# Gated DeltaNet and RWKV-7 step on one core: the first pair's key product moves among the gates' segments, and the convolution's tiles get a pool of their own

## The chip, the core and the metric

The kernel runs on one core of a Trainium2 chip. The metric is the device time of one execution in microseconds. A core has TensorE (PE in the profile; PEld are its weight loads), VectorE (DVE), ScalarE (ACT), GpSimd (POOL) and SyncE (SP), which here issues all DMAs from one queue, in order. Matrix products land in PSUM, which has eight banks; everything else lies in SBUF.

## The reference, cut to what matters

A two-layer trunk: a gated DeltaNet layer, then an RWKV-7 layer, on a prompt of 1024 + 16 tokens and on 8 sample sequences of 8 tokens, 1104 tokens in all. Only the first layer's beginning matters here.

```
xn = rmsnorm(x, norm_w)                      # 1104 tokens x 1024
proj = xn @ w_in                             # q, k, v (4096 columns), z (2048), b and a (16 + 16)
qkv, new_buf = causal_conv(qkv, conv_buf, conv_w)      # 4 taps per channel, then silu
q, k = l2norm(...), l2norm(...)              # 8 heads of 128
beta = sigmoid(b);  g = -exp(a_log) * softplus(a + dt_bias)
# per chunk of 64 tokens:
gc = cumsum(g);  decay = exp(gc_i - gc_j) for i >= j
A = I + strict_lower((k * beta) k^T * decay)
sol = triangular_solve(A, [v * beta, k * beta * exp(gc)])
# then a scan over the chunks with the state S
```

There are 8 key heads and 16 value heads, so one key head and its two value heads make a *pair* j = 0 to 7.

## The kernel before, in words

**Input.** Nine row tiles of x (128 tokens x 1024, `x0` to `x8`; the last has 80) are loaded. `input_norm` (L280) takes them in groups of two or three: sums of squares on ACT, a power on POOL, the scaling on DVE (L296). Then PE transposes each tile in eight blocks, ACT rounds the result to a high part (L305) and DVE takes the low part (L309). High and low parts lie in `xa` and `xc`, features by tokens. The x tiles lie in a pool `inp` on SBUF's right side, which is closed behind the norm.

**Products.** Every product of the projection has 128 output columns (the gates' 64) and runs over the 1104 tokens in three segments of 384, 384 and 336 (`SEGS`). A segment is 24 matmuls: 8 tiles of features by three terms (high x high, low weight x high, high x low). `product` (L438) does a segment in two halves of 12 and yields after each: a half is a *slot*. It also loads the next product's weights (`raw_weights`, L422) and splits them in segments 1 and 2 (`next_weights`: high part on ACT, low part on POOL, L87 and L91).

**Gates.** `gates` (L350) does the product of b and a in three segments, with a copy of each into `rows` (L362), yields, turns the rows into columns (`fgt`), forms beta and g with ACT and DVE, yields, makes the running sums with PE (`fgc`), yields, turns them back (`fgr`) and stores them in DRAM (`drow`). From `drow` a pair's decays E are loaded (`decays`, L649), masked on POOL (L653, L658) and turned into exponentials on ACT.

**Convolution.** `conv` (L496) is what a product hands each segment to: ACT copies the PSUM into `raw` (L546, L547, L550), multiplies by the first tap into `cvy`, and DVE adds three taps (L526). ACT takes a tanh and DVE forms the silu (L532) into K, Q or a value tile. The three old rows of the samples come from `history`: four DMAs (L475) into `hist`, a transposition on PE into the single PSUM bank `m` and a copy into `histT` (`history_turn`, L479). `hist`, `histT`, `last`, `raw` and `cvy` are tiles of the pool `gfront`, which opens when `inp` has closed and lies in the same room.

**Chain of pair 0.** From K and E come the scores (`fsc` on PE, L702 to L712 on DVE) of three segments. Their diagonal blocks of 32 go through DRAM (`ltd`, L718; `invA`, L729) into an inverse of 31 steps with two DVE instructions each (L573, L575), whose result goes through DRAM again (`g_t`, `g_u`, `T1n`) to PE's merges (`rY`, L767 the copy). Only then the scan over the chunks of pair 0 can start.

**Order.** In `layer0` (L2134) everything up to the first slot is ordered by a planner, by readiness in a simulated run and by the order in the text. From L2199 on the orders of PE and ACT are written out by hand: slots are counted, from -24 for the key product of pair 0, and `gdn_events` (L923) and `front_events` (L997) hang each step at a slot: pair 0's E is loaded at -18.5 to -18.3, its exponentials are taken from -16 on, its scores at -15.2, -14.4 and -13.6, its inverse at -11.5 and on, the merges from 2.5 on. The gates' last three parts hang at -23.4, -21.4 and -20.4. DVE, POOL and SP are ordered by the planner everywhere. All engines run their own orders strictly in sequence.

Of the kernel before, what the change touches and what calls it, by code (L numbers as in the profile page):

```python
# [14 lines left out]
D = 1024  # L15
# [21 lines left out]
class Builder:  # L37
# [229 lines left out]
    def input_open(self):  # L267
        self.inp = ExitStack()
        self.lp = self.inp.enter_context(self.tc.tile_pool(name="inp", bufs=1, side="right", reuse_waits="tile"))
        self.xrows = []  # L270

    def input_load(self, qs):
        for q in qs:
            x = self.t(self.lp, [128, D], f"x{q}")
            self.xrows.append((x, self.rows_of_x(x, q)))
            if q == 0:
                self.nwb = self.t(self.lp, [128, D], "nwb")
                self.nc.sync.dma_start(self.nwb, self.i["norm_w"][0].rearrange("(o d) -> o d", o=1).broadcast_to([128, D]))
# [71 lines left out]
    def gates(self, xh, xl):  # L350
        nc, i, t, gp = self.nc, self.i, self.t, self.gatep
        al, wz, rows, upto, past, part = self.gate_in
        nea = t(gp, [128, 16], "nea")
        self.act(nea, al[:, 0], AF.Exp)
        nc.vector.tensor_scalar(nea, nea, -1.0, None, op0=ALU.mult)
        whi = t(gp, [128, 8, 64], "whi2", dt=F32R)
        wlo = t(gp, [128, 8, 64], "wlo2", dt=F32R)
        self.split(wz, whi, wlo)
        w = ([whi[:, 0:4, :], whi[:, 4:8, :]], [wlo[:, 0:4, :], wlo[:, 4:8, :]])
        for s, (c0, n) in enumerate(SEGS):  # L360
            p = self.dense(w, 64, xh, xl, s)
            nc.scalar.copy(rows[:, c0:c0 + n], p[0:48, 0:n])  # L362
        yield
        col = self.col
        p = self.ps("f", 2, "gt")
        for k in range(9):
            self.transpose(p[:, 48 * k:48 * k + 48], rows[:, 128 * k:128 * k + 128])
        pv = p[:, 0:432].rearrange("p (k x) -> p k x", x=48)
        b, x, y, g = [t(gp, [128, 9, 16], n) for n in ("gb", "gx", "gy", "g")]
        nc.vector.tensor_tensor(x, pv[:, :, 32:48], al[:, 1].unsqueeze(1).broadcast_to([128, 9, 16]), op=ALU.add)  # L370
        nc.vector.scalar_tensor_tensor(y, x, -1.0, x, op0=ALU.mult, op1=ALU.max)
        self.act(y, y, AF.Exp, scale=-1.0)
        self.act(b, pv[:, :, 0:16], AF.Tanh, scale=0.5)
        self.act(y, y, AF.Ln, bias=1.0)
        nc.vector.scalar_tensor_tensor(y, x, 0.0, y, op0=ALU.max, op1=ALU.add)
        nc.vector.tensor_tensor(g, y, nea.unsqueeze(1).broadcast_to([128, 9, 16]), op=ALU.mult)
        gs = t(gp, [128, 9, 16], "gs")
        nc.vector.tensor_tensor(gs, g[:, 0].unsqueeze(1).broadcast_to([128, 9, 16]), part.unsqueeze(2).broadcast_to([128, 9, 16]), op=ALU.mult)
        nc.vector.tensor_scalar(col[:, :, 0, :], b, 0.5, 0.5, op0=ALU.mult, op1=ALU.add)
        yield  # L380
        flat = lambda a: a.rearrange("p k h -> p (k h)")
        p = self.ps("f", 2, "gc")
        for a, m in ((0, upto), (144, past)):
            self.mm(p[:, a:a + 16], m[0], g[:, 0])
            self.mm(p[:, a + 16:a + 144], m[1], flat(g[:, 1:9]))
        c, d = (p[:, a:a + 144].rearrange("p (k h) -> p k h", h=16) for a in (0, 144))
        gc = t(gp, [128, 144], "gc")
        nc.vector.tensor_copy(gc.rearrange("p (j k h) -> p k j h", j=8, h=2), c.rearrange("p k (j h) -> p k j h", h=2))
        e = self.ps("m", 1, "ge")
        self.mm(e[:, 0:144], self.ones, flat(gs))  # L390
        self.mm(e[:, 144:272], self.ones, flat(g[:, 1:9]))
        self.act(col[:, :, 1, :], c, AF.Identity, scale=-1.0)
        self.act(self.eglb.rearrange("p h c -> p c h"), e[:, 0:272].rearrange("p (c h) -> p c h", h=16), AF.Exp)
        self.act(col[:, :, 2, :], c, AF.Exp)
        self.act(col[:, :, 3, :], d, AF.Exp)
        yield
        p = self.ps("f", 2, "gr")
        self.transpose(p[:, 0:128], gc[:, 0:128])
        self.transpose(p[0:16, 128:256], gc[:, 128:144])
        r = t(gp, [128, 256], "gr")  # L400
        nc.vector.tensor_copy(r[:, 0:128], p[:, 0:128])
        nc.vector.tensor_copy(r[0:16, 128:256], p[0:16, 128:256])
        self.drow = self.dram([8, 9, 2, 128], "drow")
        d = self.drow.rearrange("j t h k -> (j t h) k")
        nc.sync.dma_start(d[0:128], r[:, 0:128])
        nc.sync.dma_start(d[128:144], r[0:16, 128:256])
# [62 lines left out]
    def history(self, j):  # L469

        nc, t = self.nc, self.t
        H = Ctx()
        r = t(self.fp, [108, 128], "hist", 1)[0:96]
        for u, ft in enumerate((8 + j, j, 16 + 2 * j, 17 + 2 * j)):
            nc.sync.dma_start(r[24 * u:24 * u + 24], self.i["state_gdn_conv"][0].rearrange("b r c -> (b r) c")[:, ft * 128:(ft + 1) * 128])  # L475
        H.raw = r
        return H

    def history_turn(self, H):  # L479
        p = self.ps("m", 1, "hist")  # L480
        self.transpose(p[:, 0:96], H.raw)
        H.old = self.t(self.fp, [128, 4, 8, 3], "histT", 1)
        self.nc.vector.tensor_copy(H.old.rearrange("p u b r -> p (u b r)"), p[:, 0:96])

    def last_tokens(self, j, H):
        nc = self.nc
        p = self.ps("f", 2, "last")
        self.transpose(p[0:108, 0:128], H.last.rearrange("p u b -> p (u b)"))
        ls = self.t(self.fp, [108, 128], "hist", 1)
        nc.vector.tensor_copy(ls, p[0:108, 0:128])  # L490
        for u, ft in enumerate((8 + j, j, 16 + 2 * j, 17 + 2 * j)):
            c = slice(ft * 128, (ft + 1) * 128)
            nc.sync.dma_start(self.o["s_gdn_conv"][0].rearrange("b r c -> (b r) c")[:, c], ls[27 * u:27 * u + 24])
            nc.sync.dma_start(self.o["p_gdn_conv"][0, 0][:, c], ls[27 * u + 24:27 * u + 27])

    def conv(self, H, u, ft, dst):  # L496

        nc, t = self.nc, self.t
# [2 lines left out]

        def begin():
            if u == 0:
                H.last = t(self.fp, [128, 4, 27], "last", 1)
            raws[0] = raw = t(self.fp, [128, 411], "raw", 3)
            sv = raw[:, 0:88].rearrange("p (b r) -> p b r", r=11)
            nc.vector.tensor_copy(sv[:, :, 0:3], H.old[:, u])
            nc.gpsimd.memset(raw[:, 88:91], 0.0)

        def follow(s, wd):  # L510
            prev = raws[s][:, wd:wd + 3]
            if s < 2:
                raws[s + 1] = t(self.fp, [128, 411], "raw", 3)
                nc.gpsimd.tensor_copy(raws[s + 1][:, 0:3], prev)
            else:
                nc.gpsimd.tensor_copy(H.last[:, u, 24:27], prev)

        def taps(s, wd, y):
            raw = raws[s]
            if s == 0:  # L520
                sv = raw[:, 0:88].rearrange("p (b r) -> p b r", r=11)
                nc.gpsimd.tensor_copy(H.last[:, u, 0:24].rearrange("p (b r) -> p b r", r=3), sv[:, :, 8:11])
            y.append(t(self.fp, [128, 408], "cvy", 2))
            self.act(y[0][:, 0:wd], raw[:, 0:wd], AF.Identity, scale=cw[0])
            for k in range(1, 4):
                nc.vector.scalar_tensor_tensor(y[0][:, 0:wd], raw[:, k:k + wd], cw[k], y[0][:, 0:wd], op0=ALU.mult, op1=ALU.add)  # L526
# [1591 lines left out]
    def build(self):  # L2118
        nc, tc = self.nc, self.tc
        with self.ctx as top:  # L2120
            self.input_open()
            self.input_load((0, 1, 2))
            self.consts()
# [10 lines left out]
    def layer0(self, top, right, xa, xc):  # L2134
# [7 lines left out]
        gates = ExitStack()  # L2142
        self.input_load(range(3, 9))
        self.gates_open(gates)
        self.input_norm(hi, lo)
        self.inp.close()
        self.gdn_front(front)
        self.raw_weights(1024)
        self.wnew = [], []
        self.next_weights(0)  # L2150
        self.next_weights(1)
# [2 lines left out]
        self.vectors()  # L2154
        kh, kl = [h[:, k] for h in hi for k in range(4)], [l[:, k] for h in lo for l in h for k in range(l.shape[1])]
        rows = [xa[:, k] for k in range(6)] + [xc[:, k] for k in range(10)]
        gate = self.gates(kh, kl)
        next(gate)
        G = [None] * 8

        def open_(j):
# [5 lines left out]
            self.gp = pool("gdn", ctx)  # L2167
        open_(0)
        self.history_turn(G[0].H)
        self.gdn_zero()  # L2170
        self.gdn_events(G, open_, lambda: next(gate, None), swap)

        def products():
# [12 lines left out]
                        i, h = j - 1 + h // 2, h % 2  # L2186
                        todo.append((4096 + 128 * (2 * i + h), lambda w, i=i, h=h: self.gdn_gate(i, G[i], h, kh, kl, w)))
            for n, (_, f) in enumerate(todo):
                yield from f(todo[n + 1][0] if n + 1 < len(todo) else None)

        def before(u):
            while True:
# [2 lines left out]
                    return  # L2195
                for f in self.events.pop(v):
                    f()
        before(-24)
        with tc.manual_schedule(engines={mybir.EngineType.PE, mybir.EngineType.Activation}):  # L2199
            self.slot = -24  # L2200
            for _ in products():
                before(self.slot + 1)
                self.slot += 1
        self.slot = None
        front.close()
        before(999)
        xbp = pool("xb", right, side="right")
        xb = [t(xbp, [128, 1113], f"xb{k}") for k in range(8)]
# [345 lines left out]
```

## Time and profile before

| | |
|---|---|
| three timed runs, median (lowest to highest) | 2180.25 us (2178.22 to 2181.9) |
| the profiled execution | 2173.21 us |
| its span | 2171.5 us, 54811 instructions |
| PE / DVE / ACT / POOL busy in the span | 94% / 73% / 59% / 38% |
| mean granted TensorE clock | 0.982 of full speed |
| DMA | 292.52 MB, 135 GB/s |

A page shows one profiled execution. Names like `dk<-xa,whi` are out<-in with the buffer numbers left out: `d` is the PSUM bank of a product, with `k`, `q` or `v` behind it for whose; without a letter it is here the gates'. `f`, `m` and `r` are other PSUM banks. Idle time of an engine is put down to what ended it. Matmul records overlap, since matmuls are pipelined. The times in the lines of a timeline are the start from the span's beginning and the length, and consecutive instructions of a group are merged into one line with a count.

### The profile page before, as it was taken

What the parts mean: (1) busy time and instruction counts of PE and PEld (TensorE: products, weight loads), DVE (VectorE), ACT (ScalarE), POOL (GpSimd) and SP (SyncE); (2) the same over time, 40 slices, a digit from 0 to 9 for tenths busy, and PEclk for the clock granted to TensorE, in tenths of its full rate; (3) what the DMA queues carried; (4) which work ended last, traced back from release to release, by engine and by line L of the source; (5) the groups of instructions that cost most, each with busy time, mean ns of one, the idle gap of its engine ahead of it and who ended that gap; (6) DMA issues with size and microseconds to landing.
All of it is one profiled execution on the core that took longest, in us unless ns stands there. A gap on an engine that the chain in (4) does not pass through costs nothing. (4 is left out here: it accounts for less than half of the span.)

```text
span 2171.5 us, 54811 instructions
## 1 busy us (share of the span) xinstructions
PE 2046.2 (94%) x20418; PEld 1905.8 (88%) x20418; DVE 1583.4 (73%) x4212; ACT 1283.1 (59%) x3750; POOL 834.9 (38%) x1136
## 2 busy tenths in 40 slices
PE   6969899999999999999999999889899999999997
PEld 5959899999999999998899999889798988888876
DVE  6968879698888979795334676757979557767755
ACT  4536565656565665656533365664747446677774
POOL 3523334334343333334231352344524254444444
PEclk9979999999999999999999999999999999999999
DMA  3424343424333333335345115655555486677754
GB/s 120 122 58 105 77 108 90 118 79 107 90 97 106 106 97 104 97 102 159 106 129 135 63 54 191 220 160 174 169 180 158 117 224 175 188 234 225 228 178 139
DMA packets 430724, 292.52 MB, mean 135 GB/s; under 512 B 147337, under 2 KB 413050, under 8 KB 430458
## 3 DMA queue, kind: packets, MB, share of 16 engines
q1 hardware_dynamic: 430458, 289.02, 46.2%
q8 instruction: 161, 2.64, 0.5%
q14 instruction: 105, 0.86, 0.1%
HBM read 197.55 MB, written 91.37 MB: 133 GB/s over the span
## 5 line engine op out<-in xcount | busy, mean ns | idle before, releaser
L91 POOL TENSOR_TENSOR wlo<-wraw,whi 128x512 fp32r<-128x512 f32 (+1 forms) x246 | 331.1, 1348 | 465.6 <-ACT whi L87 413.9
L77 PE MATMUL d<-xc,whi 128*128 128x384 f32 (+2 forms) x1006 | 279.5, 337 | 4.8 <-ACT whi L87 4.1
L526 DVE SCALAR_TENSOR_TENSOR cvy<-raw,cw,cvy 128x408 f32<-128x408 f32 (+2 forms) x288 | 199.0, 692 | 17.1 <-ACT cvy L63 15.7
L87 ACT CAST whi<-wraw 128x512 fp32r<-128x512 f32 (+1 forms) x246 | 149.8, 611 | 88.1 <-PE d L77 51.2
L77 PEld LDWEIGHTS d<-xc,whi 128*128 128x128 f32 (+1 forms) x1006 | 183.4, 189 | 7.8 <-ACT whi L87 4.8
L77 PE MATMUL d<-xc,wlo 128*128 128x384 f32 (+3 forms) x476 | 157.7, 340 | 2.7 <-POOL wlo L91 2.7
L77 PE MATMUL dz<-xc,whi 128*128 128x384 f32 (+1 forms) x480 | 153.9, 338 | 0.0
L77 PE MATMUL dv<-xc,whi 128*128 128x384 f32 (+1 forms) x480 | 152.4, 337 | 0.0
L77 PE MATMUL d<-xa,whi 128*128 128x384 f32 (+3 forms) x450 | 142.1, 340 | 4.5 <-ACT whi L87 1.7
L63 ACT ACTIVATE o<-rA,gcol 128x128 f32<-128x128 f32 x128 | 42.0, 366 | 116.9 <-DVE S L905 116.7
L573 DVE TENSOR_TENSOR invtmp<-invA,invT 72x31 f32<-72x31 f32 (+15 forms) x248 | 102.2, 412 | 3.2
L77 PE MATMUL dv<-xa,whi 128*128 128x384 f32 (+1 forms) x288 | 99.1, 344 | 0.0
L77 PE MATMUL dz<-xa,whi 128*128 128x384 f32 (+1 forms) x288 | 98.6, 342 | 0.0
L575 DVE TENSOR_TENSOR invT<-invT,invtmp 72x31 f32<-72x31 f32 (+15 forms) x248 | 95.0, 383 | 3.3
L77 PEld LDWEIGHTS d<-xc,wlo 128*128 128x128 f32 (+1 forms) x476 | 89.3, 189 | 6.8 <-POOL wlo L91 3.6
L77 PEld LDWEIGHTS dz<-xc,whi 128*128 128x128 f32 x480 | 89.4, 189 | 4.6 <-issue 4.5
L77 PEld LDWEIGHTS d<-xa,whi 128*128 128x128 f32 (+1 forms) x450 | 83.9, 189 | 8.2 <-issue 3.7
L77 PEld LDWEIGHTS dv<-xc,whi 128*128 128x128 f32 x480 | 89.2, 188 | 1.4 <-issue 1.4
L77 PE MATMUL d<-xa,wlo 128*128 128x384 f32 (+3 forms) x252 | 84.9, 337 | 1.4 <-POOL wlo L91 1.4
L77 PE MATMUL dk<-xc,whi 128*128 128x384 f32 (+1 forms) x240 | 79.3, 349 | 0.0
L77 PE MATMUL dq<-xc,whi 128*128 128x384 f32 (+1 forms) x240 | 77.0, 338 | 0.0
L1335 DVE SCALAR_TENSOR_TENSOR mixs<-xb,pcol,mixs 128x320 f32<-128x320 f32 (+2 forms) x96 | 68.6, 725 | 5.9 <-ACT mixs L63 5.6
(542 smaller groups left out, 6801.0 us busy)
## 6 DMA issues: line engine op xcount, KB each, us to landing
wraw<-in_gdn_w_in SPq DMA_DIRECT2D x96, 256.0 KB
wraw<-in_rwkv_w_rkvz SPq DMA_DIRECT2D x80, 256.0 KB
Sb<-in_state_gdn SPq DMA_DIRECT2D x64, 256.0 KB
sldcak<-cakd SPq DMA_DIRECT2D x24, 576.0 KB
wraw<-in_rwkv_w_o SPq DMA_DIRECT2D x42, 256.0 KB
E<-drow SPq DMA_DIRECT2D x24, 384.0 KB
attn<-drow SPq DMA_DIRECT2D x24, 384.0 KB
wraw<-in_gdn_w_out SPq DMA_DIRECT2D x36, 256.0 KB
```

The lines of the kernel that those rows point to most:

```text
L63: return self.nc.scalar.activation(out, in_, func, bias=bias, scale=scale, **kw)
L77: self.nc.tensor.matmul(out, lhsT, rhs, start=start, stop=stop)
L87: nc.scalar.copy(hi, x)
L91: e.tensor_tensor(lo, x, hi.bitcast(F32), op=ALU.subtract)
L526: nc.vector.scalar_tensor_tensor(y[0][:, 0:wd], raw[:, k:k + wd], cw[k], y[0][:, 0:wd], op0=ALU.mult, op1=ALU.add)
L573: nc.vector.tensor_tensor(tmp, A[:, j, j + 1:32].unsqueeze(2).broadcast_to([nb, n, m]), Tv[:, j, 0:m].unsqueeze(1).broadcast_to([nb, n, m] ...
L575: nc.vector.tensor_tensor(Tv[:, j + 1:32, 0:m], Tv[:, j + 1:32, 0:m], tmp, op=ALU.subtract)
L1335: nc.vector.scalar_tensor_tensor(x[:, f:], xb[:, 8 + a + f:8 + b], mu, x[:, f:], op0=ALU.mult, op1=ALU.add)
```

## The change

1. A pool `gconv` is opened ahead of everything else on the right side and stays open to the end of the DeltaNet's front; `hist`, `histT`, `last`, `raw` and `cvy` are taken from it instead of `gfront`.
2. All nine x tiles are taken when `inp` opens, not one by one as they are loaded.
3. The load of the key's weights of pair 0 stands ahead of the input's norm in the text.
4. The gates yield after each segment of their product instead of once behind the three.
5. The history's DMAs and its transposition stand ahead of the gates. The key product of pair 0 starts behind the gates' first segment: both halves of its first segment, then the gates' segments 1 and 2, then their three last parts, then the rest of the key product, all in the part that the planner orders. There its taps and silus are issued at once instead of at slots.
6. The hand-written order starts at slot -18, with the query product; the key product's six slots are gone from it, and what hung below -18 runs ahead of it. The gates' slots find nothing left to do.

```
+        self.xt = [self.t(self.lp, [128, D], f"x{q}") for q in range(9)]
...
-            x = self.t(self.lp, [128, D], f"x{q}")
+            x = self.xt[q]
...
             nc.scalar.copy(rows[:, c0:c0 + n], p[0:48, 0:n])
-        yield
+            yield
...
-        r = t(self.fp, [108, 128], "hist", 1)[0:96]
+        r = t(self.cvp, [108, 128], "hist", 1)[0:96]
...
-                H.last = t(self.fp, [128, 4, 27], "last", 1)
-            raws[0] = raw = t(self.fp, [128, 411], "raw", 3)
+                H.last = t(self.cvp, [128, 4, 27], "last", 1)
+            raws[0] = raw = t(self.cvp, [128, 411], "raw", 3)
...
-            y.append(t(self.fp, [128, 408], "cvy", 2))
+            y.append(t(self.cvp, [128, 408], "cvy", 2))
...
+            self.cvx = ExitStack()
+            self.cvp = self.cvx.enter_context(tc.tile_pool(name="gconv", bufs=1, side="right", reuse_waits="tile"))
             self.input_open()
...
         self.gates_open(gates)
+        self.raw_weights(1024)
         self.input_norm(hi, lo)
         self.inp.close()
         self.gdn_front(front)
-        self.raw_weights(1024)
...
-        gate = self.gates(kh, kl)
-        next(gate)
...
         self.history_turn(G[0].H)
+        gate, first = self.gates(kh, kl), G[0].keys(0)
+        for n in range(3):
+            next(gate)
+            if not n:
+                next(first)
+                next(first)
+        for _ in range(3):
+            next(gate, None)
+        for _ in first:
+            pass
...
             for n, (_, f) in enumerate(todo):
-                yield from f(todo[n + 1][0] if n + 1 < len(todo) else None)
+                if n:
+                    yield from f(todo[n + 1][0] if n + 1 < len(todo) else None)
...
-        before(-24)
+        before(-18)
...
-            self.slot = -24
+            self.slot = -18
...
         front.close()
+        self.cvx.close()
```

More of the change, by code (lines that the diff above doesn't have):

```diff
@@ L481, in history_turn @@
         self.transpose(p[:, 0:96], H.raw)
-        H.old = self.t(self.fp, [128, 4, 8, 3], "histT", 1)
+        H.old = self.t(self.cvp, [128, 4, 8, 3], "histT", 1)
         self.nc.vector.tensor_copy(H.old.rearrange("p u b r -> p (u b r)"), p[:, 0:96])
@@ L488, in last_tokens @@
         self.transpose(p[0:108, 0:128], H.last.rearrange("p u b -> p (u b)"))
-        ls = self.t(self.fp, [108, 128], "hist", 1)
+        ls = self.t(self.cvp, [108, 128], "hist", 1)
         nc.vector.tensor_copy(ls, p[0:108, 0:128])
@@ L512, in follow @@
             if s < 2:
-                raws[s + 1] = t(self.fp, [128, 411], "raw", 3)
+                raws[s + 1] = t(self.cvp, [128, 411], "raw", 3)
                 nc.gpsimd.tensor_copy(raws[s + 1][:, 0:3], prev)
```

## The prediction

> **What bounds the kernel now.** I read the page first, part 2.
>
> ```profile
> ## 2 busy tenths in 40 slices
> PE   6969899999999999999999999889899999999997
> DVE  6968879698888979795334676757979557767755
> ```
>
> A slice is 54.3 us. TensorE (PE) has two poor slices in the first four: the first, in which the input lands and is normed, and the third, 108.6 to 162.9 us. From then on it is at 9 nearly throughout. So I asked for the waits of 15 to 140 us, longest in total first (engine, line, what it waited for: us, times, longest), and then for the engines' busy time in stretches cut at the events found.
>
> ```profile
> PE rY L77 <- DMA T1n<-g_t: 20.6, 2, 20.0
> ```
> ```profile
> core 0: us, PE busy (x) PEld busy (x) DVE busy (x) ACT busy (x) POOL busy (x), PEclk, DMA share, GB/s
> 41.00:59.00 18.00, 17.56 (x116) 16.47 (x115) 6.71 (x17) 8.15 (x18) 1.94 (x4) 1.00 0.09 23
> 59.00:69.00 10.00, 9.93 (x61) 9.61 (x60) 9.85 (x17) 5.47 (x15) 7.33 (x14) 1.00 0.96 287
> 69.00:83.00 14.00, 12.29 (x76) 11.42 (x75) 13.76 (x56) 9.40 (x30) 8.87 (x16) 1.00 0.27 63
> 83.00:90.00 7.00, 7.00 (x72) 6.58 (x70) 6.92 (x15) 3.23 (x7) 4.22 (x4) 1.00 0.49 112
> 90.00:113.40 23.40, 22.38 (x162) 20.99 (x160) 22.85 (x60) 10.93 (x28) 10.43 (x13) 1.00 0.28 76
> 113.40:133.40 20.00, 0.00 (x0) 0.00 (x0) 14.76 (x39) 1.10 (x6) 3.03 (x3) 0.60 0.20 52
> ...
> 141.00:240.00 99.00, 97.47 (x833) 92.85 (x832) 77.98 (x227) 63.29 (x207) 35.26 (x54) 1.00 0.32 87
> ```
>
> The stall of 20 us at 113.4 is ended by the inverse of pair 0, whose blocks come back through DRAM as T1n. Ahead of it VectorE (DVE) is the full engine: of the 54.4 us from 59.0 to 113.4 it is busy 53.38. Before that, from 41 to 59 us, DVE is busy 6.71 of 18 and PE 17.56. So DVE sets the end of the stall, and it starves in 11.3 us ahead of its full strip, while PE, which feeds it, is full. After the stall PE is busy 97.47 of 99 us: what the stall's end gains, the end of the kernel gains. The timeline of DVE (start, length, what; in brackets its idle time before) shows the strip's first piece and its last.
>
> ```profile
> 40.88 0.32 DVE L309 TENSOR_TENSOR xc<-m,xc 128x160 fp32r<-128x160 f32 x1
> ...
> 46.84 0.26 DVE L483 COPY histT<-mhist 128x96 f32<-128x96 f32 x1 [3.82 <-PE mhist L74]
> ...
> 51.76 2.94 DVE L526 SCALAR_TENSOR_TENSOR cvy<-raw,cw,cvy 128x408 f32<-128x408 f32 x3 [0.17 <-ACT cvy L63]
> 54.62 0.30 DVE L388 COPY gc<-fgc 128x144 f32<-128x144 f32 x1
> ...
> 59.69 0.61 DVE L526 SCALAR_TENSOR_TENSOR cvy<-raw,cw,cvy 128x384 f32<-128x384 f32 x1
> ...
> 60.34 2.22 DVE L526 SCALAR_TENSOR_TENSOR cvy<-raw,cw,cvy 128x384 f32<-128x384 f32 x2
> ...
> 63.62 3.58 DVE L526 SCALAR_TENSOR_TENSOR cvy<-raw,cw,cvy 128x336 f32<-128x336 f32 x3
> ...
> 67.62 0.64 DVE L526 SCALAR_TENSOR_TENSOR cvy<-raw,cw,cvy 128x408 f32<-128x408 f32 x1
> ...
> 70.77 1.65 DVE L712 SCALAR_TENSOR_TENSOR E<-fsc,bp,E 128x128 f32<-128x128 f32 x6
> ...
> 89.70 0.17 DVE L573 TENSOR_TENSOR invtmp<-invA,invT 72x31 f32<-72x31 f32 x1
> ...
> 127.97 0.19 DVE L575 TENSOR_TENSOR invT<-invT,invtmp 72x31 f32<-72x31 f32 x1
> ```
>
> The last split of the input ends at 41.2, then DVE waits for the gates and for the key's history. The key's taps (cvy) of segment 0 run at 51.76, and those of the other segments keep DVE until 67.6. The first six multiplications into E, which the inverse needs, end at 70.77 + 1.65 = 72.42. The inverse runs from 89.70 to 128.16, with other taps between its steps.
>
> **The change part by part.** *The key product ahead of the hand-written order.* No matmul, tap or DMA is added or removed: the 72 matmuls, their ACT copies and the DVE taps are only free to run earlier. What PE can give is bounded by its idle time between the gates' first segment and the query's first matmul:
>
> ```profile
> 29.89 0.30 PE L74 MATMUL r<-ident,x 128*128 128x128 f32 x1 [0.28 <-DVE x L296]
> ...
> 33.12 0.39 PE L77 MATMUL d<-xc,whi 128*64 128x384 f32 x1 [0.61 <-DVE xc L309]
> ...
> 39.47 0.37 PE L77 MATMUL d<-xa,whi 128*64 128x336 f32 x1 [0.72 <-ACT xa L305]
> ...
> 47.23 0.38 PE L74 MATMUL fgt<-ident,rows 48*128 48x48 f32 x3 [0.44 <-ACT rows L362]
> ...
> 59.21 0.33 PE L77 MATMUL dq<-xa,whi 128*128 128x384 f32 x1
> ...
> 65.87 0.83 PE L77 MATMUL fsc<-K 128*128 128x128 f32 x6
> ```
>
> 0.28 + 0.61 + 0.72 + 0.44 = 2.05 us, and not a microsecond more, however early the key's first segment comes. Each gap can be filled by a key matmul whose tiles are there. I take 1.5 between 0 and 2.05, since a free order seldom fits every gap. The query product then starts at 57.7 instead of 59.21, and all of PE's hand-written order with it.
>
> DVE gains more than PE, since it is behind PE there. At 65.87 PE has the key's scores, but DVE is still in the key's taps until 67.6. Those taps move ahead of 60 us, where DVE idles: segment 0 to about 44, behind the last split, segments 1 and 2 behind their products. ACT has its share:
>
> ```profile
> 64.58 0.64 ACT L63 ACTIVATE cvy<-raw,cw 128x408 f32<-128x408 f32 x1
> ...
> 67.07 0.68 ACT L63 ACTIVATE E<-E,gcol 128x128 f32<-128x128 f32 x2
> ```
>
> The query's first tap can start when this ACT step ends, 65.22, so at 63.7 with PE 1.5 ahead. From there DVE has one tap (0.64) and then what it does in before between 67.62 and 72.42 (4.80): 63.7 + 0.64 + 4.80 = 69.1. That is 3.3 us ahead of 72.42. With PE ahead by 0 it is 1.8, by 2.05 it is 3.9. The rest of the strip is full, its work is the same, and the inverse always has a step ready, so 3.3 arrives at the stall's end and at the kernel's.
>
> *E must be there in time.* Its rows hang on the gates: gc's copy (54.62) stood behind the three taps of 51.76, which take 2.94. These go ahead, though those of segment 1 may take their place: 0 to 2.9 us earlier, and I take 1. Even at 0, E is selected on GpSimd (POOL) as it is now:
>
> ```profile
> 62.14 1.14 POOL L653 TENSOR_SCALAR_AFFINE_SELECT E<-E 128x768 f32<-128x768 f32 x1 [0.48 <-DMA E<-drow]
> ...
> 63.84 0.73 POOL L658 TENSOR_SCALAR_AFFINE_SELECT E<-E 64x64 f32<-64x64 f32 x2
> ```
>
> These end at 64.6, and the six exponentials at 0.34 each at 66.6. The multiplications would need them at 69.1 - 1.65 = 67.5. So the gates' rows cost nothing while they come at most 0.9 us later than now.
>
> *POOL beside the taps.* Five taps of 60.34 and 63.62 took 5.80 where the rows at 59.69 and 67.62 have 0.61 and 0.64, an excess of 2.8 us, all of it while POOL works on E and on weights. The forecast has the selects finished before the query's taps begin at 63.7, so the excess meets an idle DVE. If they aren't, it comes back (second rival). [...]
>
> *The pool of the convolution, the x tiles, the early weights.* These issue nothing of their own. The key's weights were already next in the queue behind the gates' small inputs (row at 20.09 below), so moving their line past the norm moves no DMA. The history's DMA is ahead of any wait on x tiles as well. What the pool buys is that taps needn't wait for the input's room. No bound on that is separate from the sum above. Against it stands room only: the input lies lower, and no copy or load grows.
>
> ```profile
> 20.09 0.98 SPq L428 DMA_DIRECT2D wraw<-in_gdn_w_in  x2
> ...
> 27.52 1.63 SPq L475 DMA_DIRECT2D hist<-in_state_gdn_conv  x4
> ```
>
> *The sum.* The profiled execution took 2173.21 us, 1.71 around its span of 2171.5; it becomes 2169.9. The three timed runs have 2180.25 as median (2178.22 to 2181.9), 7.0 above the profile; the difference is carried over: 2180.25 - 3.3 = 2176.9. About 0.2%, 4.4 us, is what a measurement can tell from no change here, and this is below it.
>
> **The rivals.** [...] DVE's order is not written out, so its meetings with POOL in the strip are dealt anew.
>
> ```profile
> 104.57 1.63 DVE L526 SCALAR_TENSOR_TENSOR cvy<-raw,cw,cvy 128x384 f32<-128x384 f32 x1
> ...
> 114.13 1.64 DVE L526 SCALAR_TENSOR_TENSOR cvy<-raw,cw,cvy 128x408 f32<-128x408 f32 x1
> ```
>
> Each of these is 1.0 above its fellows. With PE's whole 2.05 (3.9 us) and two or three such meetings fewer, the gain is 5.9 to 6.9, say 6.4: 2173.9. For it: in 113.4 to 133.4 POOL is busy 3.03 and could move. Against it: it needs luck twice.
>
> *No change: POOL meets the query's taps.* If the gates' rows are no earlier, the selects run from 62.1 on beside taps from 63.7 on, and the 2.8 return: 3.3 - 2.8 = 0.5, 2179.8. For it: the selects' time today. [...]
>
> *Slower: the history's transposition holds PE.* It is now written ahead of the gates, so it may stand on PE ahead of x tiles 3 to 8. Its PSUM slot is free once x tile 2 is split, and its DMA lands later (second row: the queue waited 1.9 us behind the issue, 29.15 + 1.9 = 31.05):
>
> ```profile
> 24.58 0.42 DVE L309 TENSOR_TENSOR xc<-m,xc 128x256 fp32r<-128x256 f32 x1
> ```
> ```profile
> SPq L475 <- DMA hist<-in_state_gdn_conv: 1.9, 1, 1.9
> ```
>
> PE could stand from 25.0 to 31.05, 6.05 us, with the gates' product and six x tiles behind it. The wait swallows PE's gaps, so only the 1.8 of DVE's reordering is left: 6.05 - 1.8 = 4.25 slower, 2184.5; at worst, with that lost too, 2186.3. It decides from 1.8 us of waiting on. Against it: the x transposes have high priority, and an order that foresees the landing puts it later.
>
> *Nothing moves.* The free order may keep the key product behind the gates' third segment, as PE had it: 2180.25.
>
> **How the numbers follow.** Forecast 0.46 (its own range 1.8 to 5, as the gates' rows and one lock may help; 0.08 of it beyond 4.4), faster rival 0.27, POOL's meeting 0.08, the held PE 0.16 (0.10 beyond 4.4), nothing 0.03. Faster: 0.08 + 0.27 = 0.35. Slower: 0.10. Same: 0.38 + 0.08 + 0.06 + 0.03 = 0.55. The likeliest is 2176.9. The range goes from 2172.0 (a gain of 8.2, the faster rival with the runs' spread) to 2183.0 (2.8 slower); left out are some 0.05 below and 0.15 above.
>
> **What would show it.** Right: dk matmuls between the gates' first and second segment (before 42 us); key taps at about 42 to 46; the query's first matmul at 57 to 58; first E multiplications done by about 69; DVE full from there; T1n's wait ending at about 130 instead of 133.4, as long a wait or nearly. Wrong: an mhist on PE with idle time of microseconds before it; E multiplications waiting for ACT's exponentials; taps of 1 us or more beside POOL from 62 us on; or DVE idle before the inverse's first step, its DMA not landed. If the stall's end moves and the kernel's end doesn't, a later wait took it, and the sum was wrong in carrying 3.3 to the end.

## The result, and the profile after

The changed kernel takes 2185.4 us (median; 2179.28 to 2192.23), beside 2179.79 us for the kernel before. The ratio is 1.0027, 95% interval [1.0018, 1.0036]: 5.9 us slower (3.9 to 7.8). I had forecast 2176.9 us and a range that ends at 2183.0.

First the waits of the changed kernel from 15 to 140 us, in the columns of the prediction's list (its line numbers are one higher than before's).

```profile
PE rY L77 <- DMA T1n<-g_t: 18.4, 2, 17.9
...
ACT E L63 <- POOL E L659: 8.0, 1, 8.0
...
POOL E L654 <- DMA E<-drow: 7.3, 2, 7.0
...
PE fsc L77 <- DVE E L713: 6.4, 1, 6.4
...
DVE E L713 <- ACT E L63: 3.9, 3, 3.1
...
DVE invtmp L574 <- DMA invA<-ltd: 2.1, 1, 2.1
```

Read from POOL's line: POOL waits for the rows of E, ACT for POOL, DVE for ACT, and PE for DVE. In the kernel before these waits were 0.5 (POOL) and 1.1 (PE), and ACT and DVE had none here. The busy times of the changed kernel, over the prediction's stretches:

```profile
core 0: us, PE busy (x) PEld busy (x) DVE busy (x) ACT busy (x) POOL busy (x), PEclk, DMA share, GB/s
41.00:59.00 18.00, 18.00 (x117) 16.93 (x117) 8.49 (x20) 8.36 (x15) 2.58 (x7) 1.00 0.07 19
59.00:69.00 10.00, 8.77 (x56) 8.20 (x54) 7.21 (x28) 2.57 (x8) 0.39 (x2) 1.00 0.13 47
69.00:83.00 14.00, 7.69 (x32) 7.37 (x32) 9.86 (x36) 9.18 (x26) 11.00 (x20) 0.76 0.72 202
83.00:90.00 7.00, 7.00 (x42) 6.97 (x43) 3.59 (x11) 3.41 (x12) 1.76 (x4) 1.00 0.38 95
90.00:113.40 23.40, 22.48 (x189) 20.84 (x188) 22.92 (x58) 10.78 (x27) 10.72 (x13) 1.00 0.31 86
```

The early strip is as meant: PE has no gap from 41 to 59, DVE does 8.49 where it did 6.71. Then comes what I hadn't foreseen: from 59 to 90 DVE is busy 20.66 of 31 us (30.52 before, 12.61 up to 72 and 17.91 behind it), and PE 7.69 of 14 from 69 to 83. The strip that was full has holes of 10 us.

The chain that makes them, picked from the timelines of PE, DVE, SP (SPq), POOL and ACT of the changed kernel, in order of time:

```profile
42.15 0.25 PE L74 MATMUL mhist<-ident,hist 96*128 96x96 f32 x1
...
43.68 2.00 DVE L527 SCALAR_TENSOR_TENSOR cvy<-raw,cw,cvy 128x408 f32<-128x408 f32 x3 [0.77 <-ACT cvy L63]
...
45.24 0.57 PE L74 MATMUL fgt<-ident,rows 48*128 48x48 f32 x6
...
49.42 0.39 PE L74 MATMUL fgt<-ident,rows 48*128 48x48 f32 x3
...
49.84 0.31 DVE L371 TENSOR_TENSOR gx<-fgt,al 128x144 f32<-128x144 f32 x1 [2.55 <-PE fgt L74]
...
54.23 0.33 PE L77 MATMUL dq<-xa,whi 128*128 128x384 f32 x1
...
54.47 1.40 DVE L377 TENSOR_TENSOR g<-gy,nea 128x144 f32<-128x144 f32 x1
...
56.50 0.61 PE L77 MATMUL fgc<-g,upto 128*128 128x16 f32 x4
...
58.32 0.56 DVE L533 SCALAR_TENSOR_TENSOR K<-raw,cvy 128x384 f32<-128x384 f32 x1 [1.71 <-ACT raw L63]
58.80 1.77 DVE L527 SCALAR_TENSOR_TENSOR cvy<-raw,cw,cvy 128x336 f32<-128x336 f32 x3
60.48 0.30 DVE L389 COPY gc<-fgc 128x144 f32<-128x144 f32 x1
...
63.36 0.65 DVE L527 SCALAR_TENSOR_TENSOR cvy<-raw,cw,cvy 128x408 f32<-128x408 f32 x1 [1.67 <-ACT cvy L63]
63.92 0.28 DVE L402 COPY gr<-fgr 128x128 f32<-128x128 f32 x1
...
64.23 0.36 SPq L406 DMA_DIRECT2D drow<-gr  x1
...
69.94 0.87 POOL L654 TENSOR_SCALAR_AFFINE_SELECT E<-E 128x768 f32<-128x768 f32 x1 [7.04 <-DMA E<-drow]
...
71.34 0.69 ACT L63 ACTIVATE E<-E,gcol 128x128 f32<-128x128 f32 x2 [8.02 <-POOL E L659]
...
71.78 0.64 DVE L713 SCALAR_TENSOR_TENSOR E<-fsc,bp,E 128x128 f32<-128x128 f32 x2 [3.14 <-ACT E L63]
...
89.91 0.19 DVE L574 TENSOR_TENSOR invtmp<-invA,invT 72x31 f32<-72x31 f32 x1 [2.13 <-DMA invA<-ltd]
...
131.49 0.19 DVE L576 TENSOR_TENSOR invT<-invT,invtmp 72x31 f32<-72x31 f32 x1
```

The same links in the kernel before, from its timelines (E's select, at 62.14, and the last fgt, at 47.23, stand in the prediction):

```profile
47.66 0.31 DVE L370 TENSOR_TENSOR gx<-fgt,al 128x144 f32<-128x144 f32 x1 [0.35 <-PE fgt L74]
...
51.88 0.60 PE L77 MATMUL fgc<-g,upto 128*128 128x16 f32 x4
...
55.74 0.29 DVE L401 COPY gr<-fgr 128x128 f32<-128x128 f32 x1 [0.82 <-PE fgr L74]
...
56.06 0.36 SPq L405 DMA_DIRECT2D drow<-gr  x1
```

The gates' chain is one after the other: nine transpositions, gx, two ACT steps, g, the sums fgc, gc, fgr, gr, the store, the load. The planner, which now orders the key product among them, put key matmuls (45.74 to 49.42) between the sixth and the seventh transposition. Between gx and fgc ACT copies and multiplies the key's second segment (50.74 and 51.34) ahead of the chain's second ACT step, DVE has a tap ahead of g, and g itself takes 1.40 us instead of 0.31 while POOL splits weights (54.27 to 55.70). A silu and three taps of the key stand ahead of gc on DVE. Ahead of gr stand a silu of the key and a tap of the query, which waits for ACT and holds gr behind it. Every piece put between is short, but gx is 2.2 us later than before, fgc 4.6, gc 5.9, gr 8.2, E's select 7.8. The rest follows in ACT's written order: the query's copies stand behind the exponentials, so they wait the 8.02 us too. Taps that have nothing to work on leave DVE idle, and they come back between the inverse's steps: it starts 0.2 us later than before and takes 41.8 us instead of 38.5, with 19 taps and 23 other instructions between its steps instead of 16 and 19. T1n's wait ends at 137.05 (133.43 before).

### The profile page after: what moved, and what is told of

It reads as the page before. It is cut to its first block, busy times and chain, and to the rows that moved or that the text cites. A ratio compares the mean times of both kernels' runs of the same rounds, so it can differ in the third digit from the quotient of the medians.

```text
span 2181.3 us, 54818 instructions
## 1 busy us (share of the span) xinstructions
PE 2052.1 (94%) x20418; PEld 1909.7 (88%) x20418; DVE 1574.7 (72%) x4212; ACT 1284.1 (59%) x3750; POOL 838.0 (38%) x1136
## 5 line engine op out<-in xcount | busy, mean ns | idle before, releaser
L527 DVE SCALAR_TENSOR_TENSOR cvy<-raw,cw,cvy 128x408 f32<-128x408 f32 (+2 forms) x288 | 192.2, 667 | 19.9 <-ACT cvy L63 18.4
L1336 DVE SCALAR_TENSOR_TENSOR mixs<-xb,pcol,mixs 128x320 f32<-128x320 f32 (+2 forms) x96 | 68.5, 724 | 5.2 <-ACT mixs L63 4.9
```

Source lines behind the costliest of these rows:

```text
L1336: nc.vector.scalar_tensor_tensor(x[:, f:], xb[:, 8 + a + f:8 + b], mu, x[:, f:], op0=ALU.mult, op1=ALU.add)
```

## The experiments

A profile is one execution, and its input lands earlier or later than in another: the first scaling on DVE starts between 11.95 us (e8) and 13.87 (e9), at 13.34 in the kernel before, 12.59 in the changed one and 12.21 in e4. Two profiles of the changed kernel have T1n's wait end at 137.05 and 135.85. E's select is the start of POOL's first one; T1n is the start of the first rY behind the stall.

| kernel | E's select | T1n | ratio to before, 95% |
|---|---|---|---|
| before | 62.1 | 133.4 | 1 |
| changed | 69.9 | 137.1 | 1.0027 [1.0018, 1.0036] |
| e1_pool_only | 61.8 | 133.1 | 1.0002 [0.9987, 1.0016] |
| e2_gates_first | 70.6 | 137.9 | 1.0031 [1.0014, 1.0049] |
| e3_gates_priority | 70.9 | 137.9 | 1.0018 [1.0004, 1.0031] |
| e4_order_by_hand | 60.5 | 130.2 | 0.9982 [0.9968, 0.9997] |
| e5_late_gates_alone | 68.3 | 135.2 | 0.9993 [0.9977, 1.0010] |
| e6_by_hand_late_gates | 68.3 | 135.0 | 1.0005 [0.9988, 1.0022] |
| e7_by_hand_no_pool | 62.7 | 133.0 | 0.9983 [0.9970, 0.9996] |
| e8_by_hand_exps_behind | 58.7 | 129.8 | 0.9977 [0.9965, 0.9989] |
| e9_two_hops | 66.1 | 132.2 | 0.9989 [0.9976, 1.0003] |
| e10_four_hops | 69.7 | 136.5 | 0.9996 [0.9984, 1.0008] |
| e11_late_gates_late_exps | 67.3 | 137.4 | 1.0019 [1.0002, 1.0035] |
| e12_exps_behind_no_pool | 59.6 | 130.1 | 0.9985 [0.9967, 1.0003] |
| e13_changed_early_rows | 39.1 | 133.8 | 1.0003 [0.9986, 1.0020] |
| e14_changed_again | 69.1 | 135.9 | 1.0024 [1.0006, 1.0041] |
| e15_before_early_rows | 39.7 | 132.3 | 0.9991 [0.9975, 1.0008] |

**The pool alone.** e1 keeps the first three points of the change and takes the rest back:

```
-        before(-18)
+        before(-24)
...
-                if n:
-                    yield from f(...)
+                yield from f(...)
```

> The kernel before with the convolution's pool, the x tiles taken at once and the early weights, and with the old order of gates and key product. Late gates (the key's steps stand between the gates' steps, so E comes 7.8 us later): nothing is reordered, so the ratio to before is 1.000 within 0.001, E's first select is at about 62 and the wait for T1n ends at about 133.4. Room (the new pool and the x tiles' places cost): 1.0027, or at least half of that, with E's first select still at 62.

E's select, T1n and the time are those of the kernel before: no cost of the pool, the x tiles and the early weights shows (0.4 us, between 2.8 less and 3.5 more).

**Another order from the text or by priority.** e2 puts all gates ahead of the key product in the text, e3 gives the gates' last three parts a high priority:

```
-        for n in range(3): next(gate); ... next(first) ...
+        for _ in gate: pass
```
```
+            with tc.high_priority():
+                next(gate, None)
```

> The changed kernel with all the gates' parts ahead of the key product in the text. The planner still puts 62 key matmuls ahead of the gates' sums (36 in before, 72 and 13 query matmuls in the changed kernel). Late gates: E's first select falls between the two, at 64 to 68, and so does the time, ratio 1.000 to 1.002. Room: 1.0027 as the changed kernel, wherever E's select stands.

> The changed kernel with the gates' last three parts at high priority. The planner's order hardly moves: the sums still stand behind 72 key and 13 query matmuls. Late gates: E's first select at 68 to 71, ratio 1.002 to 1.0035, as the changed kernel. A priority that is enough to bring the gates forward would give a select at 62 or below and a ratio of 1.000 or less.

e2 missed: E's select didn't fall between the two kernels, it came at 70.6. e3 came out as expected at the select, with a ratio just below the expected range. In both E is as late as in the changed kernel. I put that down to the planner, which goes by when a step's operands are there, and key matmuls are always there.

**The order by hand.** e4 leaves the key's first segment among the gates' segments and writes the rest out from slot -22 (the events are the gates' last three parts):

```
-        for _ in range(3):
-            next(gate, None)
-        for _ in first:
-            pass
...
-                if n:
-                    yield from f(...)
+                yield from f(...) if n else first
...
-        before(-18)
+        before(-22)
...
-        for u in (-23.4, -21.4, -20.4):
+        for u in (-22.5, -20.6, -19.6):
```

> The key's first segment stays among the gates' segments, and the hand-written order begins behind it: the nine turnings of the gates' rows, two key halves, the sums, one key half, the turning back, one key half, then the query. Late gates: E's first select at 60 to 62, PE's query from 56, the first six multiplications into E done at 67 to 69 (72.4 before, 74.7 in the changed kernel), the wait for T1n ends at 128 to 130, ratio 0.9965 to 0.999. Room, or an early key product that harms by itself: 1.002 to 1.003 as the changed kernel.

Timelines of e4, POOL and DVE:

```profile
60.52 0.87 POOL L654 TENSOR_SCALAR_AFFINE_SELECT E<-E 128x768 f32<-128x768 f32 x1 [3.60 <-DMA E<-drow]
...
66.85 1.64 DVE L713 SCALAR_TENSOR_TENSOR E<-fsc,bp,E 128x128 f32<-128x128 f32 x6
...
124.75 0.19 DVE L576 TENSOR_TENSOR invT<-invT,invtmp 72x31 f32<-72x31 f32 x1
```

The first six multiplications end at 68.5 (72.4 before), the inverse 3.2 us earlier, T1n's wait at 130.24 (0.2 beyond the expected range), and the kernel is 3.9 us faster than before (0.7 to 7.0). Up to 1.1 of the 3.2 us at T1n can be the input, which landed that much earlier in this profile. With the gates in time, the early key product gives a gain of about the size that was forecast.

**Late gates with either order.** e5 is the kernel before, e6 is e4, each with the gates' last three parts some two slots later and E's loads from -17.5:

```
-        for u in (-23.4, -21.4, -20.4):      # e5
+        for u in (-21.4, -19.4, -17.6):
...
-        for u in (-22.5, -20.6, -19.6):      # e6
+        for u in (-20.5, -18.6, -17.6):
```

> The kernel before, with only the gates' last three parts moved two to three slots later in the order written out (from -23.4, -21.4, -20.4 to -21.4, -19.4, -17.6) and pair 0's loads of E from -18.5 to -17.5. The key product, the pool, the x tiles stay as in the kernel before. Theory (the late E alone costs the time): E's select on POOL starts at 67 to 69 us instead of 62.1, the first multiplications into E end at about 74 instead of 72.4, the wait for T1n ends at 134.5 to 136.5 instead of 133.4, and the ratio to the kernel before is 1.0003 to 1.0015. Rival (the changed kernel is slow for the room, or for the taps in the free part, not for E): E late, T1n's wait within 0.5 us of 133.4, ratio 1.000.

> The order by hand of e4_order_by_hand (key's first segment among the gates' segments, the rest written out), with the gates' last three parts two slots later than there and the loads of E from -18.5 to -17.5: the gain of the early key taps and the loss of the late E in one kernel. Theory (the late E takes what the early taps give): E's select at about 66 us against 60.5, the first multiplications into E wait for ACT's exponentials and end at 71 to 73, the wait for T1n ends at 132.5 to 134.5 against 130.2, ratio 0.9995 to 1.0005. Rival (the gates' time does not matter, the order by hand does): T1n's wait ends at 130 to 131, ratio 0.998.

In e6, T1n is 4.8 us later than in e4, 0.5 us beyond the expected range; the ratio is 0.0023 higher, as expected, but the two intervals overlap. e5 moved T1n by 1.8 as expected, though its first six multiplications end at 72.6 and not at about 74. Its ratio missed the expected 1.0003 to 1.0015: 1.5 us below before (from 5.0 below to 2.2 above) neither shows the loss nor excludes it.

**Late rows alone.** e9 and e10 send the gates' rows through two and four more DMA copies. No compute engine has another instruction, but E comes later, and so does what stands behind the store in SP's queue: in e10 the states, attn and a load of weights are issued 8.7, 8.6 and 10.5 us later than in e4.

```
+        for n in range(2):                   # e10: 4
+            r2 = t(gp, [128, 256], f"hop{n}")
+            nc.sync.dma_start(r2[:, 0:128], r[:, 0:128])
+            nc.sync.dma_start(r2[0:16, 128:256], r[0:16, 128:256])
+            r = r2
         nc.sync.dma_start(d[0:128], r[:, 0:128])
```

> The order by hand of e4_order_by_hand with the gates' rows gr sent through two more copies in SBUF by DMA ahead of their store into drow: the loads of E come later by two landings, some 4 us, and no compute engine has an instruction more. A dose of the late E and of nothing else. Theory (E has about 2 us of slack in e4_order_by_hand, then each microsecond of a late E is lost): E's select at about 64.5 us against 60.5, the first multiplications into E end 2 to 3 us later, T1n's wait ends at 131.5 to 133.5 against 130.2, ratio 0.9990 to 0.9998 against 0.9982. Rival (E's time does not matter, the order does): T1n's wait within 0.5 us of 130.2, ratio 0.998.

> As e9_two_hops with four copies: E comes some 8 us later than in e4_order_by_hand, about as late as in the changed kernel, with the key product's steps as early as there. Theory: E's select at about 68.5 us, ACT waits for it with the query's copies behind it, T1n's wait ends at 135 to 138, ratio 1.0005 to 1.003, so that the changed kernel's loss is reproduced by a late E alone. Rival: T1n's wait at 130 to 131, ratio 0.998.

The waits of e10, which repeat those of the changed kernel:

```profile
PE rY L77 <- DMA T1n<-g_t: 18.3, 2, 17.9
ACT E L63 <- POOL E L664: 8.8, 1, 8.8
POOL E L659 <- DMA E<-drow: 8.5, 2, 8.1
...
PE fsc L77 <- DVE E L718: 5.9, 1, 5.9
DVE E L718 <- ACT E L63: 4.1, 2, 3.8
```

Against e4, E 5.6 us later moves T1n by 1.9, and 9.2 later by 6.3: from some 4 us on, each microsecond costs a little over one at the stall's end. (In both, 0.6 and 1.0 us of the shift stand in gx already, ahead of the copies.) e10 repeats the changed kernel's inverse too: 41.85 us, with the same 19 taps and 23 other instructions between its steps, where e4 has 38.4 us, 16 and 19. e9's T1n is in the expected range, e10's too. So late rows alone bring the stall's end to where the changed kernel has it. The time doesn't follow as far. The ratios rise in the same order, 0.9982, 0.9989, 0.9996, but their intervals overlap, and e10 stays below the 1.0005 to 1.003 that I expected: the changed kernel's whole loss in time is not reproduced.

**The exponentials moved behind the query's steps.** e11 is e6 with pair 0's exponentials and scores 0.8 to 1.2 slots later:

```
-[-16, -15.2, -14.4], [-15.2, -14.4, -13.6]
+[-14.8, -14.4, -13.9], [-14.0, -13.6, -13.2]
```

> As e6_by_hand_late_gates, where E comes late, with pair 0's exponentials and scores 0.8 to 1.2 slots later in the orders written out for ACT and PE, so that ACT's copies of the query stand ahead of the wait for E and not behind it. Theory (the loss is the query's steps held behind the wait on ACT, so that VectorE idles): VectorE is fuller from 59 to 72 us than there (7.55 of 13), T1n's wait ends 1 to 3 us earlier than there (135.0), ratio 0.9990 to 1.0003. Rival (the chain from E through the scores to the inverse is what counts, not what stands behind the wait): T1n's wait at 134.5 to 136, ratio 1.0005.

Wrong on every count, for the rival too: T1n is 2.4 us later, DVE isn't fuller from 59 to 72 us (7.35), and PE now waits longer ahead of its scores (waits of e11 and of e6, one line each):

```profile
PEld fsc L77 <- DVE E L713: 7.9, 1, 7.9
```
```profile
PEld fsc L77 <- DVE E L713: 2.9, 1, 2.9
```

The wait only changed its place, so moving the steps around it doesn't help.

**The pool again, and a better order.** e7 is e4, and e12 is e8, without the pool and without the x tiles at once. e8 is e4 with ACT's four steps on the gates' columns behind the copy of gr:

```
-        self.act(col[:, :, 1, :], c, AF.Identity, scale=-1.0)     # and the three behind it
         yield
...
         nc.vector.tensor_copy(r[0:16, 128:256], p[0:16, 128:256])
+        self.act(col[:, :, 1, :], c, AF.Identity, scale=-1.0)     # and the three behind it
```

> The order by hand of e4_order_by_hand without the convolution's own pool and without taking the x tiles at once: the convolution's tiles lie in the pool that opens when the input's has closed, as in the kernel before. Theory (the pool buys nothing, the order is all): within 0.7 us of e4_order_by_hand at T1n's wait, 130.2, ratio 0.9975 to 0.9990. Rival (the taps of the key's first segment wait for the input's room): these taps start at 46 us or later instead of 43 to 44, T1n's wait ends 1 to 3 us later, ratio 0.999 to 1.000.

> The order by hand of e4_order_by_hand, with the exponentials and the copies of the gates' columns on ACT (gcol, eglb: L393 to L396) written behind the last copy of the gates' rows, so that the key's taps of segment 1 come sooner on DVE. Theory (DVE still starves for ACT ahead of the strip): E's select within 0.5 us of 60.5, the first multiplications into E end up to 1 us earlier, T1n's wait ends at 129.2 to 130.2, ratio 0.997 to 0.998. Rival (E or the strip sets it, not these steps): the same as e4_order_by_hand, 0.998, T1n at 130.2 or up to 0.5 later.

> The order of e8_by_hand_exps_behind without the convolution's own pool and without taking the x tiles at once. If the pool buys nothing: T1n's wait within 1.5 us of 129.8, ratio within 0.0012 of 0.9977. If the key's first taps wait for the input's room: they start 1 to 2 us behind the last split instead of beside it, T1n's wait ends 1.5 to 3 us later, ratio 0.9985 to 0.9995.

e8 is the fastest, 0.9977 [0.9965, 0.9989], 5.0 us below the kernel before, with DVE's taps of segment 1 at 50.71 instead of 54.54; that it beats e4 lies within the intervals. E's select came 1.8 us earlier than in e4, which wasn't expected, and the first multiplications ended 0.4 later (68.9) and not earlier. In the profiles without the pool the key's first taps start 2 to 3 us later (46.10 and 44.45, with it 43.26 and 42.52), T1n 2.8 and 0.4 later, of which 0.4 and 0.7 can be the input. So e7 has the rival's T1n and the theory's ratio, and e12 is as expected if the pool buys nothing; the ratios differ by 0.0001 and 0.0008, less than they are known to. What the pool is worth stays open between nothing and some 3 us.

**The late rows taken out of the changed kernel.** In e13 and e15 pair 0's decays come from a constant that is in DRAM early (the gates' sums for pair 0 are left out of E and attn; all gate steps still run):

```
+        z = t(gp, [18, 128], "z")
+        nc.gpsimd.memset(z, -4000.0)
+        self.drow0 = self.dram([1, 9, 2, 128], "drow0")
+        nc.sync.dma_start(self.drow0.rearrange("j t h k -> (j t h) k"), z)
...
-                          self.drow[j, 3 * s:3 * s + 3]...
+                          (self.drow if j else self.drow0)[j, 3 * s:3 * s + 3]...
```

> The changed kernel with pair 0's E and attn rows loaded from a constant that is stored in DRAM early, so that pair 0 has constant decays instead of the gates' running sums; gates, copies, stores and all else are kept, and later pairs read the gates' rows. Theory (the loss is the late E): E's select before 60 us, the first multiplications into E end by 69, T1n's wait ends at 130 to 131.5 (137.05 in the changed kernel), ratio 0.9975 to 0.9990. Rival (something else of the changed order costs time, behind the stall): T1n's wait at 130 to 132 all the same, but the ratio stays at 1.0005 to 1.002.

> The changed kernel itself, beside e13_changed_early_rows on one chip: E's select at about 70, T1n's wait at 136.5 to 138, ratio 1.0018 to 1.0036 as in its first runs. If it comes out below 1.0012, the gap to e10_four_hops was chance.

> The kernel before with pair 0's rows from the same early constant. There VectorE is in the key's taps until 67.6 us, so an earlier E buys nothing: T1n's wait ends at 132.4 to 134, ratio 0.9992 to 1.0005. If E's arrival set the time there, the first multiplications would end before 71.5 us and the wait before 132.4.

e14 is slower than before, like the first runs, with T1n 0.7 us earlier than I expected. e15 bears out that an earlier E buys little in the kernel before: T1n comes 1.2 us earlier, 0.1 more than expected, and 0.3 of it can be the input. e13 missed both its expectations. Without the late E 2183.86 becomes 2180.15 (the intervals overlap), and T1n comes 2.1 us earlier than in e14 (3.3 than in the first profile). But it stays 3.5 us behind e4's (0.6 of it can be the input), so E's own lateness is only a part of what the late rows cost at the stall. What is late next, from the waits of e13 between 58 and 95 us:

```profile
POOL attn L658 <- DMA ltd<-E: 7.2, 1, 7.2
ACT raw L551 <- PE dv L77: 6.4, 1, 6.4
...
PE dv L77 <- POOL wlo L91: 2.7, 1, 2.7
```

POOL stands at the select of attn, and the low part of the next weights (wlo), for which PE waits, is queued behind it. The profile puts the end of POOL's wait to ltd's stores. SP's timeline of e13 shows what was issued when:

```profile
64.47 0.35 SPq L410 DMA_DIRECT2D drow<-gr  x1
64.91 0.38 SPq L411 DMA_DIRECT2D drow<-gr  x1
66.34 0.38 SPq L433 DMA_DIRECT2D wraw<-in_gdn_w_in  x1
66.78 1.60 SPq L1095 DMA_DIRECT2D Sb<-in_state_gdn  x3
68.48 0.92 SPq L654 DMA_DIRECT2D attn<-drow  x2
69.81 1.98 SPq L723 DMA_DIRECT2D ltd<-E  x4
```

The store of the late gates' rows still holds SP's queue, and behind it stand the load of weights (66.34; 58.33 in e4), the states, attn (60.75 in e4) and ltd. That this makes up the 3.5 us is read from the profile, and was not tried by itself.

## Why the prediction was wrong, point by point

**The step that failed** is "E must be there in time". I put the gates' rows "0 to 2.9 us earlier", took 1, and added that they "cost nothing while they come at most 0.9 us later than now". E came 7.8 us later. I had looked at one link alone, gc's copy behind DVE's taps, as if the other links stood still. With the key product free, each link met key, query or weight work that was ready first. The bound was too narrow on the late side, because a step that nobody holds in place has none from the order before. In its place the runs show: in the order by hand T1n comes at 130.2 with the rows in time (e4) and at 136.5 with the rows sent late (e10), 0.5 from the changed kernel's. Of this, E itself carries some 2 to 3 us (e13 beside the changed kernel's two profiles). The 3.5 between e13 and e4 stay when E is early; the DMAs queued behind the late store are their likely way, not tried by itself.

**The 0.9** was mis-sized too. The changed kernel shows 1.84 us from E's select (69.94) to the first multiplication (71.78) when nothing else is awaited; in e4 there are 6.33, so 4.5 us of room, and e9 and e10, with some 4, agree. The 7.8 went past any such room.

**DVE's gain** didn't come in the changed kernel. In e4, where the rows are in time, it did: 3.3 forecast, 3.2 at T1n (2.1 if the earlier input is taken off) and 3.9 in time (0.7 to 7.0). The key's taps came at 43.68, as forecast.

**PE's bound** was wrong: 2.05 us "and not a microsecond more", but the query's first matmul came at 54.23, 5.0 earlier. The gaps were filled, yet an idle sum bounds only what PE gains with the same work ahead. Here the gates' sums and their transposition, ahead of the query's first matmul in the kernel before, went behind it (PE is busy 37.92 us ahead of it instead of 39.97), and 0.75 us came from an input that landed earlier in this profile (12.59 instead of 13.34).

**POOL's meeting with the taps** didn't occur in the changed kernel: the query's three taps from 63.36 on run at 0.62 to 0.65 each, with POOL idle from 62.9 to 69.94, where E's first select starts. No run shows a lock between DVE and POOL, one of which the forecast's own range takes in. What the rows show is that some DVE steps took longer beside POOL's: the five taps of the kernel before, with their excess of 2.8 us, and here g, with 1.40 us instead of 0.31. **The history** held nothing: its transposition ran at 42.15 between two gates' matmuls without a wait. **The pool** shows no cost (e1).

**The slower rival** had the right side and about the size (4.25), by the wrong mechanism. The signs that came true were two others on my list: the E multiplications waiting for ACT's exponentials (3.14), and DVE idle before the inverse's first step (2.13).

**Carrying the stall's end to the kernel's end** holds roughly: over the seventeen rows of the table a line through the time against T1n has a slope of 1.17 (standard error 0.18, correlation 0.86), with 1.9 us scatter. By it 3.6 us at the stall make some 4 of the changed kernel's 5.9. e10, with T1n 0.5 us short of the changed kernel's, takes 2.2 to 11.3 us less by the ends of the two intervals. e14 came at 1.0024, above the 1.0012 below which I would have called this gap chance. The profiles point to a further loss behind the stall: from the first rY<-T1n of pair 0 to the last of pair 7 the changed kernel's two take 854.0 and 854.9 us, the fifteen others 849.7 to 853.1 (851.4 before, 852.3 in e10). What makes it, and whether it is all of the gap, stays open.

## What to carry to other kernels

When work that is always ready is set free beside a chain of short steps on several engines, follow that chain link by link: the filler gets in at each one, and a text order or a priority need not keep it out. Ask for each freed step which late operand stands at its end and how much room it has, and who stands behind it in each in-order queue, DMA issues included (a load of weights issued at 66.34 behind the late store in e13, at 58.33 in e4). A written-out order with the filler placed between the chain's links (e4, e8) kept the gain.

## What the runs showed of the hardware

PE lost more than its wait of 6.4 us. The windows of the changed kernel around it, with the granted clock behind POOL's column:

```profile
67.70:74.16 6.46, 0.07 (x1) 0.00 (x0) 2.76 (x12) 2.81 (x9) 3.90 (x7) 0.90 0.96 288
74.16:79.00 4.84, 4.84 (x19) 4.84 (x20) 4.04 (x14) 4.84 (x15) 3.20 (x7) 0.50 0.86 242
79.00:81.00 2.00, 2.00 (x11) 2.00 (x11) 1.92 (x8) 1.21 (x4) 1.89 (x2) 0.81 0.20 28
```

Behind the wait PE ran at half the clock for about 5.6 us, so I estimate that some 2.8 us of work more were lost, half of that. Whether this moved the stall's end isn't shown: PE still stands 17.9 us at T1n. The half clock had begun within the wait, at 72.9, and lasted 6.8 us, to 79.7. The wait's length alone doesn't decide. In e5 PE waited 2.10 us at the same place, until 72.69, and lost the clock as well, for 3.4 us in all (its windows):

```profile
72.69:75.00 2.31, 2.31 (x10) 2.31 (x11) 1.48 (x9) 2.31 (x8) 0.86 (x3) 0.50 0.95 332
...
76.00:76.50 0.50, 0.50 (x5) 0.50 (x4) 0.50 (x4) 0.50 (x3) 0.50 (x3) 0.93 0.31 45
```

In e6 and e9, with waits of 2.6 and 2.8 us there, it stayed at 1.00. By the windows of the profiles the half clock lasts about 6.8 us at this place in five of them (the changed kernel's two, e2, e10, e11), 3.4 in e5 and e7, and 3.4 in e13, some 6 us later there. In the clock records of the kernel before and of the changed one every stretch of half clock, but the last, which the end cuts off, is a whole multiple of 3.41 us, from 3.41 to 23.89. Why the 2.10 us of e5 went with a loss of the clock and the 2.8 of e9 did not is not shown.

These five profiles are among the six latest at T1n (135.9 and later; all others 135.2 and earlier); the clock of the sixth, e3, was not read at this place. What the clock adds there beside the late rows is not separated by any run.
